# A decoder trunk on one core: two weight sums recorded later, and one block product moved up in the last up unit

## The chip, the cores and the metric

The kernel runs on one core of one Trainium2 chip. The metric is the device time of one execution in microseconds (us); for a kernel it is the median of its runs.

## What is computed

Two decoder layers over 1024 positions of width 1024, in float32. Each layer has a token mixer with four memory cross-attention heads beside it, an output projection, and a dense MLP:

```
def squared_relu_mlp(h, w_up, w_down):
    a = jax.nn.relu(h @ w_up)
    return (a * a) @ w_down
...
        x = x + jnp.concatenate([mix, cross], axis=-1) @ w_o[i]
        x = x + squared_relu_mlp(rmsnorm(x, mlp_norm_g[i]), mlp_w_up[i], mlp_w_down[i])
    return rmsnorm(x, final_norm_g)
```

`w_up` is 1024 x 4096 and `w_down` 4096 x 1024. Layer 0 has latent attention, layer 1 sliding-window attention; the change touches only the MLPs.

## The kernel before

**Precision.** TensorE multiplies operands that are rounded to float32r. Each float32 operand is split into a high part (ScalarE copies it into a float32r tile, line 99) and a low part (VectorE subtracts the high part, line 100), and each product is made of three matmuls: high by high, high by low, low by high (lines 1700 to 1702 in the up product, 2053 to 2055 in the down product).

**Strassen.** Both MLP products run as Strassen's seven block products on 2 x 2 blocks. The up product (function `mlp`) goes through 16 units `i` of 256 hidden columns. For a unit the raw weights come by two DMAs (`load_raw`, line 1619), are scaled by the norm's gain on ScalarE (`gain_w`, line 1592), and are combined on VectorE (`sum_w`): s1 = a21+a22 (line 1635), s2 = s1-a11 (1636), a21 = a11-a21 (1637) and s4 = a12-s2 (1638). `sums[i]` gives product `p` its weight block; `prep_w(i, p)` splits it, and `up_mm(i, p)` runs its twelve matmuls.

- Products 1, 6, 7 and 4 of a unit add up in the bank `psu`, products 2, 5 and 3 in a bank `psv`. `evac` copies `psu` out after products 1 and 6 and `psv` after product 5 (ScalarE, line 1743), since the later results need these values alone. The next product into that bank waits for the copy.
- After products 2, 7 and 3 VectorE adds a saved copy (line 1756) and squares (1735, in layer 1's first two units 1732 and 1733 on ScalarE). Products 3 and 4 end with sums of the hidden blocks (1766 to 1768 and 1748, 1751), and each block is written to DRAM (`hd`, line 1738). Line 1748 is the last reader of `psu`.
- There are two `psu` slots. Unit i+2 waits for line 1748 of unit i, and the second down tile `psy` takes the slot of the last unit.

**The order of the products.** `seq` lists (unit, product). The first two units go in turn through 6, 5, 7, 3, 4 (their products 1 and 2 ran earlier). Every later unit goes 1, 2, 6, 5, 7, 3, 4. The operand of product 6 (`X[6]`) lies in the tile `f0`, that of product 5 in `f1`; that of products 1 and 2 in `q0` and `q1`. Matmul rows name these tiles `mqf` (f0, f1) and `mqq` (q0, q1).

**From up to down.** In the last unit `dn.begin(p)` follows each product: after product 6 it loads the first eight down weight blocks into `f0` (four DMAs of 512 KB, line 1859), after product 5 the next eight into `f1`. A load waits until the last matmul that reads its tile has ended. The down product (class `Down`) then goes through (product, 256 rows) steps of 24 matmuls, with operands split four steps ahead.

**What sets the order.** The lines above are the order in which work is *recorded*. A scheduler then places each recorded instruction in its engine's queue by its own estimates of when the inputs are there, with earlier recorded work first among those that are ready. Each engine and the DMA queue of SP (SyncE) then works strictly in queue order. So moving a few lines can reorder neighbours that the lines don't name.

The lines that the prediction follows:

```
            G(a21, a11, a21, SUB)
            G(s4, a12, s2, SUB)
...
        seq += [(i, p) for i in range(2, NP) for p in (1, 2, 6, 5, 7, 3, 4)]
...
            go(i, p, ready.pop((i, p)))
            if i == NP - 1:
                dn.begin(p)
```

Of the kernel before, what the change touches and what calls it, by code (L numbers as in the profile page):

```python
# [55 lines left out]
def trunk(  # L56
# [39 lines left out]
    def split(src, hi, lo, scale=None):  # L96

        if scale is None:
            r = nc.scalar.activation(hi, src, AF.Copy)  # L99
            return r, nc.vector.tensor_tensor(lo, src, f32(hi), ALU.subtract)  # L100
        else:
            nc.scalar.activation(hi, src, AF.Copy, scale=scale)
            nc.vector.scalar_tensor_tensor(lo, src, scale, f32(hi), ALU.mult, ALU.subtract)
# [845 lines left out]
    def units_of(h):  # L949
        return units if h < H - 1 else units_end  # L950
# [153 lines left out]
    seq = [(h, u) for h in range(H) for u in units_of(h)]  # L1104
# [78 lines left out]
    NP = FF // 256  # L1183
    TORD = list(range(NT))
    SUB = ALU.subtract

    def k4(ap):
        return ap.rearrange("p (k c) -> p k c", k=4)
# [419 lines left out]
    def mlp(layer, m, early_w=None, early_mm=None):  # L1608

        X, xr = m.X, m.xr  # L1610
        V, G = nc.vector, nc.vector.tensor_tensor
# [6 lines left out]
            for h in range(2):  # L1618
                nc.sync.dma_start(out=r[h], in_=wsrc[:, 4 * h : 4 * h + 4, 256 * i : 256 * i + 256])

        ss = []

        def gain_w(i):
            for h in range(2):
# [2 lines left out]
        def sum_w(i):  # L1627
            if i < 2:
                ss.append([m.t(f"i{j}")[:, 0, :] for j in (1, 3, 5)] if i == 0 else [*[m.t("d2")] * 2, m.t("i7")[:, 0, :]])
                if i == 1:  # L1630
                    ss[1][0:2] = [ss[1][0][:, j, :] for j in range(2)]
            r = raws.pop(i)
            a11, a12, a21, a22 = r[0][:, :, 0:P], r[1][:, :, 0:P], r[0][:, :, P:256], r[1][:, :, P:256]
            s1, s2, s4 = [k4(a) for a in ss[i % 2]]
            G(s1, a21, a22, ALU.add)
            G(s2, s1, a11, SUB)
            G(a21, a11, a21, SUB)
            G(s4, a12, s2, SUB)
            sums[i] = {1: a11, 2: a12, 3: s4, 4: a22, 5: s1, 6: s2, 7: a21}

        def pair(t_):
# [21 lines left out]
        def prep_w(i, p):  # L1663
            a = sums[i][p]
            n = hct[0]
            hct[0] += 1
            if n < 7:
                hl.append([k4(v) for v in opens[n]()])
            hi, lo = hl[n % 7]
            split(a, hi, lo)  # L1670
            return hi, lo
# [6 lines left out]
        def prep_x(p, cols=range(4)):  # L1678
            for j in cols:
                c = slice(j * P, (j + 1) * P)  # L1680
                if layer and (p != 6 and j < 2 or len(cols) == 4):
                    if j % 2:
                        continue
                    c = slice(j * P, (j + 2) * P)
                src = m.t2[j] if p == 6 else xr[{5: 0, 7: 1, 4: 2, 3: 3}[p]][:, :, c]
                hi, lo = [v[:, :, c] for v in X[p]]
                split(src, hi, lo)
# [83 lines left out]
                write(7, i, h)  # L1771

        seq = [(i, p) for p in (6, 5, 7, 3, 4) for i in range(2)]
        seq += [(i, p) for i in range(2, NP) for p in (1, 2, 6, 5, 7, 3, 4)]
        LA = 4
        ready = {}

# [14 lines left out]
        else:  # L1792
            gain_w(0)
        sum_w(0)
        prep_x(6, range(3))
        load_raw(1)
# [5 lines left out]
        with tc.issue_after(m.last_n.ins):  # L1802
            gain_w(1)
        sum_w(1)
        ready[(1, 6)] = prep_w(1, 6)
        prep_x(5, (3,))
        ready[(0, 5)] = prep_w(0, 5)
        X[7] = [m.t("g0", F32R), m.t("g1", F32R)]
        X[3] = [m.t("g2", F32R), m.t("g3", F32R)]
        with tc.issue_after(m.last_n.ins):  # L1810
# [8 lines left out]
        for n, (i, p) in enumerate(seq):  # L1819
            for q_ in seq[n : n + LA]:  # L1820
                if q_ not in ready:
                    ready[q_] = prep_w(*q_)
            if (i, p) == (1, 7):
                load_raw(2)
                gain_w(2)
                sum_w(2)
            if p == 4 and 0 < i < NP - 2:
                load_raw(i + 2)
            if p == 2 and i < NP - 1:
                gain_w(i + 1)  # L1830
            if p == 6 and 2 <= i < NP - 1:
                sum_w(i + 1)
# [3 lines that stand above are left out]
# [341 lines left out]

    jw, early = {}, []
    mlp(0, m0, lambda: jw.update(early_w()), early_mm)
    m0.rp.release()  # L2180
    kv1p = pool("kv1p")
# [183 lines left out]
    m1 = Mlp(1, x1)  # L2365
    wo_strassen(1, wq, [f0, f1], m1)
    mlp(1, m1)
    m1.rp.release()
    m1.s.release()
# [35 lines left out]
```

## Time and profile before

| | us |
|---|---|
| median of 3 runs | 2110.15 |
| the runs | 2110.25, 2110.15, 2108.54 |
| the profiled execution, its own time | 2112.17 |
| its span (first to last instruction) | 2110.5 |
| TensorE busy in the span | 2071.6 (98%) |
| VectorE busy | 1493.9 (71%) |
| ScalarE busy | 1142.9 (54%) |

The profiled execution took 2.02 us more than the median and 1.7 us more than its own span. "Busy" counts an instruction from its start to its end; since matmuls overlap, TensorE can show 98% while single waits of a microsecond remain.

### The profile page before, as it was taken

Reading aid. Unit: us, or ns where it says so; the run is one execution under the profiler, and the core shown is the slowest. Engines: PE = TensorE matmul, PEld = TensorE weight load, DVE = VectorE, ACT = ScalarE, POOL = GpSimd, SP = SyncE. Lnnn points to the kernel's source line nnn. Section 1 sums busy time; section 2 is a strip of 40 time slices with the busy share of each in tenths; the row PEclk is TensorE's granted clock in tenths of the full one; section 3 lists DMA queues with packets and bytes.
Section 4 is the critical chain, followed back from the end, with each engine's and each line's share of the span. In section 5 each row is a group of like instructions: output and inputs, shape, how many; then the busy total and the mean of one; then the engine's idle time right before and its main releaser. Section 6 shows DMA issues by size and latency. Waiting matters only on the chain.

```text
span 2110.5 us, 29217 instructions
## 1 busy us (share of the span) xinstructions
PE 2071.6 (98%) x9880; PEld 1699.8 (81%) x9880; DVE 1493.9 (71%) x2876; ACT 1142.9 (54%) x2461; POOL 204.7 (10%) x288
## 2 busy tenths in 40 slices
PE   7999999999999999999999999999999999999998
PEld 6988778778778888788888878778788887888887
DVE  7555688865977766797667543897976775976565
ACT  5445477776744453444445553877845443444452
POOL 0013100000000000031111231631000000000000
PEclk9999999999999999999999999999999999999999
DMA  7202123343254445976653211146344446844332
GB/s 247 68 1 76 46 63 90 105 146 100 96 184 146 139 154 195 325 254 205 212 165 95 75 31 30 41 156 234 122 152 146 165 140 225 316 152 154 117 119 90
DMA packets 181632, 294.47 MB, mean 140 GB/s; under 512 B 18557, under 2 KB 74346, under 8 KB 181482
## 3 DMA queue, kind: packets, MB, share of 16 engines
q1 hardware_dynamic: 171008, 264.25, 38.9%
q0 software_dynamic: 8048, 25.70, 3.5%
q10 hardware_dynamic: 2426, 2.65, 0.4%
q8 instruction: 78, 1.28, 0.2%
q14 instruction: 72, 0.59, 0.1%
HBM read 194.81 MB, written 85.25 MB: 133 GB/s over the span
## 4 chain that ended last, share of the span: by engine, by line
PE 76%; DVE 8%; DMA 8%; ACT 5%; issue 2%; SPq 0%; POOL 0%; DVEq 0%; ACTq 0%; POOLq 0%
PE psy L2053 5%; PE psy L2055 5%; PE psy L2054 5%; PE psz L2054 4%; PE psz L2053 4%; PE psz L2055 4%; PE pss L964 4%; PE pso L1006 3%; PE psu L1700 3%; PE psu L1702 3%; PE psu L1701 3%; DMA mr<-in_mlp_w_up_dram 3%; DMA d<-in_mlp_w_up_dram 3%; PE psf L108 2%; PE psf L110 2%; PE psf L109 2%
## 5 line engine op out<-in xcount | busy, mean ns | idle before, releaser
L1592 ACT ACTIVATE mr<-mr,gcol 128x256 f32<-128x256 f32 (+1 forms) x160 | 67.7, 479 | 79.0 <-DMA mr<-in_mlp_w_up_dram 64.4
L2053 PE MATMUL psy<-g 128*128 128x512 f32 x256 | 99.9, 390 | 0.0
L2054 PE MATMUL psy<-g 128*128 128x512 f32 x256 | 99.6, 389 | 0.0
L2055 PE MATMUL psy<-g 128*128 128x512 f32 x256 | 99.3, 389 | 0.0
L1592 ACT ACTIVATE d<-d,gcol 128x256 f32<-128x256 f32 x128 | 57.3, 499 | 75.5 <-DMA d<-in_mlp_w_up_dram 65.4
L99 ACT ACTIVATE g<-i 128x512 fp32r<-128x512 f32 x79 | 49.6, 628 | 88.3 <-PE psz L2054 41.2
L99 ACT ACTIVATE i<-mr 128x512 fp32r<-128x512 f32 x86 | 54.0, 628 | 68.6 <-PE psz L2054 20.0
L985 ACT ACTIVATE p<-pss 128x512 f32<-128x512 f32 x108 | 63.6, 593 | 41.1 <-PE pss L964 41.0
L100 DVE TENSOR_TENSOR g<-i,g 128x512 fp32r<-128x512 f32 x79 | 55.6, 704 | 40.7 <-ACT g L99 40.6
L99 ACT ACTIVATE uh<-i 128x512 fp32r<-128x512 f32 x66 | 41.6, 630 | 76.9 <-PE psy L2054 35.7
L100 DVE TENSOR_TENSOR pl<-p,ph 128x512 fp32r<-128x512 f32 (+1 forms) x96 | 61.6, 651 | 27.6 <-ACT ph L99 27.1
L839 DVE TENSOR_REDUCE m<-psx 128x1 f32<-128x128 f32 (+5 forms) x96 | 70.2, 748 | 11.0 <-PE psx L835 10.8
L2053 PE MATMUL psz<-g 128*128 128x512 f32 x192 | 74.7, 389 | 0.0
L2054 PE MATMUL psz<-g 128*128 128x512 f32 x192 | 74.7, 389 | 0.0
L2055 PE MATMUL psz<-g 128*128 128x512 f32 x192 | 74.7, 389 | 0.0
L100 DVE TENSOR_TENSOR uh<-i,uh 128x512 fp32r<-128x512 f32 x66 | 45.5, 689 | 36.7 <-ACT uh L99 36.7
L100 DVE TENSOR_TENSOR i<-mr,i 128x512 fp32r<-128x512 f32 x78 | 53.6, 687 | 21.2 <-ACT i L99 21.0
L99 ACT ACTIVATE ph<-p 128x512 fp32r<-128x512 f32 (+1 forms) x96 | 56.4, 599 | 1.3
L1928 DVE TENSOR_TENSOR mqf<-mqq,mqf 128x512 f32<-128x512 f32 x64 | 43.0, 687 | 19.3 <-DMA mqq<-in_mlp_w_down_dram 19.2
L2055 PEld LDWEIGHTS psy<-g 128*128 128x128 f32 x256 | 48.0, 188 | 10.0
L2053 PEld LDWEIGHTS psy<-g 128*128 128x128 f32 x256 | 48.1, 188 | 9.9
L2054 PEld LDWEIGHTS psy<-g 128*128 128x128 f32 x256 | 48.1, 188 | 9.8
(746 smaller groups left out, 6972.8 us busy)
## 6 DMA issues: line engine op xcount, KB each, us to landing
i<-hd SPq DMA_DIRECT2D x154, 256.0 KB
hd<-uh SPq DMA_DIRECT2D x76, 256.0 KB
hd<-ul SPq DMA_DIRECT2D x76, 256.0 KB
mr<-in_mlp_w_up_dram SPq DMA_DIRECT2D x36, 512.0 KB
hd<-x SPq DMA_DIRECT2D x72, 256.0 KB
mr<-hd SPq DMA_DIRECT2D x70, 256.0 KB
d<-in_mlp_w_up_dram SPq DMA_DIRECT2D x32, 512.0 KB
mqq<-in_mlp_w_down_dram SPq DMA_DIRECT2D x32, 512.0 KB
```

The source lines that it names most:

```text
L99: r = nc.scalar.activation(hi, src, AF.Copy)
L100: return r, nc.vector.tensor_tensor(lo, src, f32(hi), ALU.subtract)
L839: nc.vector.reduce_max(m8s[h][:, i : i + 1], ps[:, c], axis=AX, negate=True)
L964: return lambda: nc.tensor.matmul(o, a, b, skip_group_check=True, **kw)
L985: nc.scalar.activation(p, ps, AF.Exp, scale=SC)
L1006: mms.append(lambda: nc.tensor.matmul(o, a, b, skip_group_check=True, **kw))
L1592: nc.scalar.activation(w[:, k, :], w[:, k, :], AF.Copy, scale=g_mlp[layer][:, k0 + k : k0 + k + 1])
L1700: nc.tensor.matmul(ps, wh[:, k, :], xh[:, k, :], start=p in (1, 2, 5) and k == 0, stop=False, skip_group_check=True)
L1701: nc.tensor.matmul(ps, wh[:, k, :], xl[:, k, :], start=False, stop=False, skip_group_check=True)
L2053: nc.tensor.matmul(ps, ah[:, j, :], bh, start=p in (1, 5, 2) and k == 0, stop=False, skip_group_check=True)
L2054: nc.tensor.matmul(ps, ah[:, j, :], bl, start=False, stop=False, skip_group_check=True)
L2055: nc.tensor.matmul(ps, al[:, j, :], bh, start=False, stop=k == NP - 1, skip_group_check=True)
```

## The change

In the first up unit (i = 0, in both layers) the last two weight sums, lines 1637 and 1638, are no longer recorded in `sum_w` but kept and recorded later: after the splits for products 6 of units 0 and 1 and product 5 of unit 0. In the last up unit (i = 15) the products go 1, 6, 2, 5, 7, 3, 4 instead of 1, 2, 6, 5, 7, 3, 4.

```diff
@@ sum_w @@
             G(s1, a21, a22, ALU.add)
             G(s2, s1, a11, SUB)
-            G(a21, a11, a21, SUB)
-            G(s4, a12, s2, SUB)
+
+            def rest():
+                G(a21, a11, a21, SUB)
+                G(s4, a12, s2, SUB)
+
+            if i:
+                rest()
+            else:
+                held.append(rest)
@@ mlp @@
         seq = [(i, p) for p in (6, 5, 7, 3, 4) for i in range(2)]
-        seq += [(i, p) for i in range(2, NP) for p in (1, 2, 6, 5, 7, 3, 4)]
+        seq += [(i, p) for i in range(2, NP) for p in ((1, 2, 6, 5, 7, 3, 4) if i < NP - 1 else (1, 6, 2, 5, 7, 3, 4))]
...
         ready[(0, 5)] = prep_w(0, 5)
+        held[0]()
         X[7] = [m.t("g0", F32R), m.t("g1", F32R)]
```

Line numbers after the change are 2 to 8 higher: 1637 and 1638 become 1639 and 1640; 1700 to 1702 become 1707 to 1709; 1738, 1748, 1756 and 1766 become 1745, 1755, 1763 and 1773; 1859 becomes 1867.

In the queues, layer 0 is unchanged on every engine up to its last up unit. The layers' last units change in the same way; layer 0's is shown. On PE, `psu_15` takes product 1 (weights `i_0_99`, `i_0_100`, operand `mqq`) and then product 6 (operand `mqf`), `psv_15_2` product 2. Before:

```order
L1701 MATMUL psu_15_7849<-mqq_0_32_5152,i_0_99_5819 128x512
L1702 MATMUL psu_15_7849<-mqq_0_32_5152,i_0_100_5820 128x512
L1700 MATMUL psv_15_2_7865<-mqq_0_33_5153,i_0_101_5823 128x512
L1701 MATMUL psv_15_2_7865<-mqq_0_33_5153,i_0_101_5823 128x512
L1702 MATMUL psv_15_2_7865<-mqq_0_33_5153,i_0_102_5824 128x512
L1700 MATMUL psv_15_2_7865<-mqq_0_33_5153,i_0_101_5823 128x512
L1701 MATMUL psv_15_2_7865<-mqq_0_33_5153,i_0_101_5823 128x512
L1702 MATMUL psv_15_2_7865<-mqq_0_33_5153,i_0_102_5824 128x512
L1700 MATMUL psv_15_2_7865<-mqq_0_33_5153,i_0_101_5823 128x512
```

Now:

```order
L1708 MATMUL psu_15_7849<-mqq_0_32_5152,i_0_99_5819 128x512
L1709 MATMUL psu_15_7849<-mqq_0_32_5152,i_0_100_5820 128x512
L1707 MATMUL psv_15_2_7885<-mqq_0_33_5153,x_0_105_5871 128x512
L1708 MATMUL psv_15_2_7885<-mqq_0_33_5153,x_0_105_5871 128x512
L1709 MATMUL psv_15_2_7885<-mqq_0_33_5153,x_0_105_5871 128x512
L1707 MATMUL psv_15_2_7885<-mqq_0_33_5153,x_0_105_5871 128x512
L1708 MATMUL psv_15_2_7885<-mqq_0_33_5153,x_0_105_5871 128x512
L1707 MATMUL psu_15_7849<-mqf_0_78_5664,i_0_101_5823 128x512
L1708 MATMUL psu_15_7849<-mqf_0_78_5664,i_0_101_5823 128x512
```

Five of product 2's twelve matmuls still stand between products 1 and 6; the other seven follow product 6, and then product 5.

On SP, in the same unit: `mqf_0_138` is f0 with the first eight down blocks, `mqf_0_139` f1, `mqq_0_149` a further down block, and `hd_4817<-x` the write of product 2's result. Before:

```order
L1859 DMA mqq_0_149_7987<-in_mlp_w_down_dram 128x2x512
L1918 DMA i_0_143_7925<-hd_4817 128x512
L1738 DMA hd_4817<-x_0_111_5995 128x512
L1859 DMA mqq_0_149_7987<-in_mlp_w_down_dram 128x2x512
L1859 DMA mqf_0_138_7896<-in_mlp_w_down_dram 128x2x512 x4
L1859 DMA mqf_0_139_7917<-in_mlp_w_down_dram 128x2x512 x4
L1738 DMA hd_4820<-x_0_111_5995 128x512
```

Now:

```order
L1867 DMA mqq_0_149_7987<-in_mlp_w_down_dram 128x2x512
L1926 DMA i_0_143_7925<-hd_4817 128x512
L1867 DMA mqf_0_138_7878<-in_mlp_w_down_dram 128x2x512 x4
L1745 DMA hd_4817<-x_0_111_5995 128x512
L1867 DMA mqf_0_139_7917<-in_mlp_w_down_dram 128x2x512 x4
L1745 DMA hd_4820<-x_0_111_5995 128x512
```

The write and the second `mqq` load no longer stand ahead of f0's four loads; the second `mqq` load comes some 35 rows later. On ScalarE the first split of f0 (`i_0_165<-mqf`) now also stands ahead of the copy of product 5 (`i_0_77<-psv_15_5`), which it followed before.

On VectorE, the same unit, from the third split of a down operand to line 1748 (`ul_106<-psu_15`), which frees the slot for `psy`. Before:

```order
L100 TENSOR_TENSOR g_0_167_8018<-mqf_0_138_7896,g_0_167_8018 128x512
L1756 TENSOR_TENSOR x_0_111_5995<-psv_15_5_7903,i_0_76_5662 128x512
L100 TENSOR_TENSOR g_0_168_8023<-i_0_141_7923,g_0_168_8023 128x512
L1735 SCALAR_TENSOR_TENSOR x_0_111_5995<-x_0_111_5995 128x512
L100 TENSOR_TENSOR g_0_168_8023<-mqf_0_138_7896,g_0_168_8023 128x512
L1766 TENSOR_TENSOR uh_82_5697<-x_0_111_5995 128x512
L100 TENSOR_TENSOR g_0_169_8028<-i_0_142_7924,g_0_169_8028 128x512
L1767 TENSOR_TENSOR uh_82_5697<-uh_82_5697,x_0_111_5995 128x512
L1768 TENSOR_TENSOR x_0_111_5995<-x_0_111_5995 128x512
L1748 TENSOR_TENSOR ul_106_5918<-psu_15_7849,ul_106_5918 128x512
```

Now (line 1755 is the former 1748):

```order
L1742 SCALAR_TENSOR_TENSOR x_0_111_5995<-x_0_111_5995 128x512
L100 TENSOR_TENSOR g_0_167_8018<-mr_140_7922,g_0_167_8018 128x512
L100 TENSOR_TENSOR g_0_167_8018<-mqf_0_138_7878,g_0_167_8018 128x512
L1763 TENSOR_TENSOR x_0_111_5995<-psv_15_5_7903,i_0_76_5662 128x512
L100 TENSOR_TENSOR g_0_168_8023<-mqf_0_138_7878,g_0_168_8023 128x512
L1742 SCALAR_TENSOR_TENSOR x_0_111_5995<-x_0_111_5995 128x512
L100 TENSOR_TENSOR g_0_169_8028<-i_0_142_7924,g_0_169_8028 128x512
L1773 TENSOR_TENSOR uh_82_5697<-x_0_111_5995 128x512
L1755 TENSOR_TENSOR ul_106_5918<-psu_15_7849,ul_106_5918 128x512
```

Lines 1767 and 1768 no longer come ahead of it, and the split `g_0_168<-i` has moved further up; on PE six matmuls into the second `psy` tile have moved up from the 15th place of the down product to the 8th.

In layer 1 the beginning of the up product changes too. On SP, `mr_81` and `mr_82` are the two halves of unit 2's raw weights, `d_86` and `d_87` those of unit 3. Before:

```order
L1619 DMA mr_81_13653<-in_mlp_w_up_dram 128x4x256
L1619 DMA mr_82_13654<-in_mlp_w_up_dram 128x4x256
L1619 DMA d_1_86_13755<-in_mlp_w_up_dram 128x4x256
L1738 DMA hd_4820<-ul_80_13646 128x512
L1619 DMA d_1_87_13756<-in_mlp_w_up_dram 128x4x256
```

Now:

```order
L1619 DMA mr_81_13653<-in_mlp_w_up_dram 128x4x256
L1619 DMA d_1_86_13755<-in_mlp_w_up_dram 128x4x256
L1745 DMA hd_4820<-ul_80_13646 128x512
L1619 DMA mr_82_13654<-in_mlp_w_up_dram 128x4x256
L1619 DMA d_1_87_13756<-in_mlp_w_up_dram 128x4x256
```

The second half of unit 2 now stands behind unit 3's first half and behind the write of unit 0's product 7 (`hd_4820<-ul_80`). On VectorE, from the sums of unit 2 (1635 to 1638) to line 1748 of unit 0 (`x_1_85<-psu_0`); `psv_0_5` and `psv_1_5` hold product 3 of units 0 and 1, `i_1_76` is the low part for unit 2's product 2. Before:

```order
L1635 TENSOR_TENSOR i_1_58_13467<-mr_81_13653,mr_82_13654 128x512
L1756 TENSOR_TENSOR uh_83_13699<-psv_0_5_13602,i_1_49_13385 128x512
L1636 TENSOR_TENSOR i_1_59_13468<-i_1_58_13467,mr_81_13653 128x512
L1637 TENSOR_TENSOR mr_81_13653<-mr_81_13653 128x4x128
L1638 TENSOR_TENSOR i_1_60_13469<-mr_82_13654,i_1_59_13468 128x512
L1756 TENSOR_TENSOR ul_84_13703<-psv_1_5_13618,i_1_50_13386 128x512
L1766 TENSOR_TENSOR uh_83_13699<-uh_83_13699,ul_80_13646 128x512
L100 TENSOR_TENSOR i_1_76_13560<-mr_82_13654,i_1_75_13559 128x512
L1767 TENSOR_TENSOR ul_84_13703<-uh_83_13699,uh_56_13437 128x512
L1768 TENSOR_TENSOR uh_83_13699<-uh_56_13437,uh_83_13699 128x512
L1766 TENSOR_TENSOR x_1_85_13727<-ul_84_13703,ul_80_13646 128x512
L1748 TENSOR_TENSOR x_1_85_13727<-psu_0_13410,x_1_85_13727 128x512
```

Now:

```order
L1635 TENSOR_TENSOR i_1_58_13467<-mr_81_13653,mr_82_13654 128x512
L1636 TENSOR_TENSOR i_1_59_13468<-i_1_58_13467,mr_81_13653 128x512
L1639 TENSOR_TENSOR mr_81_13653<-mr_81_13653 128x4x128
L1640 TENSOR_TENSOR i_1_60_13469<-mr_82_13654,i_1_59_13468 128x512
L1773 TENSOR_TENSOR uh_83_13699<-uh_83_13699,ul_80_13646 128x512
L1773 TENSOR_TENSOR x_1_85_13727<-ul_84_13703,ul_80_13646 128x512
L1774 TENSOR_TENSOR ul_84_13703<-uh_83_13699,uh_56_13437 128x512
L1775 TENSOR_TENSOR uh_83_13699<-uh_56_13437,uh_83_13699 128x512
L1774 TENSOR_TENSOR x_1_85_13727<-x_1_85_13727,uh_56_13437 128x512
L1775 TENSOR_TENSOR ul_84_13703<-uh_56_13437,ul_84_13703 128x512
L100 TENSOR_TENSOR i_1_76_13560<-mr_82_13654,i_1_75_13559 128x512
L1755 TENSOR_TENSOR x_1_85_13727<-psu_0_13410,x_1_85_13727 128x512
```

The rows of product 3 (1763 for `psv_0_5` and `psv_1_5`) now stand directly ahead of these twelve, all four sums of unit 2 behind them, and the split `i_1_76` is the eleventh of the twelve instead of the eighth. On PE, unit 2 of layer 1 now begins with two matmuls of product 2, two of product 5 and three of product 2, ahead of its product 1.

## Rows read from the trace of the kernel before

**Rows 1.** Waits on PE, whole span: us in total, times, longest.

```profile
PE psu L1700 <- ACT d L1743: 3.3, 7, 1.4
PE psy L2053 <- DVE ul L1748: 2.0, 2, 1.0
```

**Rows 2.** Timeline of PE, layer 0's last unit: start, us, ..., [idle before <-releaser].

```profile
840.17 0.39 PE L1700 MATMUL psu<-mqf,x 128*128 128x512 f32 x1
842.89 0.39 PE L1700 MATMUL psv<-mqf,x 128*128 128x512 f32 x1
...
851.35 0.50 PE L1700 MATMUL psu<-x,d 128*128 128x512 f32 x1
...
854.25 0.39 PE L2053 MATMUL psy<-i,i 128*128 128x512 f32 x1
...
858.57 0.50 PE L2053 MATMUL psy<-i,i 128*128 128x512 f32 x1 [0.99 <-DVE ul L1748]
```

**Rows 3.** Timeline of ACT, the same stretch.

```profile
837.96 0.58 ACT L1743 ACTIVATE d<-psu 128x512 f32<-128x512 f32 x1
845.87 0.60 ACT L1743 ACTIVATE i<-psv 128x512 f32<-128x512 f32 x1 [2.12 <-PE psv L1702]
849.34 0.63 ACT L99 ACTIVATE i<-mqf 128x512 fp32r<-128x512 f32 x1 [2.87 <-DMA mqf<-in_mlp_w_down_dram]
```

**Rows 4.** Timeline of DVE, the same stretch.

```profile
850.00 0.69 DVE L100 TENSOR_TENSOR i<-mqf,i 128x512 fp32r<-128x512 f32 x1 [8.22 <-ACT i L99]
...
857.83 0.68 DVE L1748 TENSOR_TENSOR ul<-psu,ul 128x512 f32<-128x512 f32 x1
```

**Rows 5.** Timeline of SP's DMA queue, the same stretch.

```profile
841.81 0.32 SPq L1738 DMA_DIRECT2D hd<-x  x1
842.18 0.43 SPq L1859 DMA_DIRECT2D mqq<-in_mlp_w_down_dram  x1
843.08 5.82 SPq L1859 DMA_DIRECT2D mqf<-in_mlp_w_down_dram  x8
```

**Rows 6.** Windows: length, busy us of PE, PEld, DVE, ACT, POOL; PEclk, DMA share, GB/s.

```profile
843.00:849.00 6.00, 6.00 (x28) 4.96 (x27) 0.00 (x0) 1.20 (x2) 0.00 (x0) 1.00 0.90 301
1496.00:1498.00 2.00, 2.00 (x7) 1.52 (x6) 2.00 (x4) 2.00 (x3) 0.00 (x0) 0.50 0.00 0
```

**Rows 7.** Timeline of PE, layer 1's last unit and first down step.

```profile
1793.82 0.50 PE L1700 MATMUL psu<-x,d 128*128 128x512 f32 x1 [0.31 <-DVE x L1756]
1801.03 0.50 PE L2053 MATMUL psy<-i,i 128*128 128x512 f32 x1 [1.03 <-DVE ul L1748]
```

**Rows 8.** Timeline of PE, units 0 to 2: layer 0, then layer 1.

```profile
582.43 0.50 PE L1700 MATMUL psu<-mqq,i 128*128 128x512 f32 x1 [0.42 <-DVE x L1748]
...
1494.59 0.49 PE L1700 MATMUL psu<-mqf,i 128*128 128x512 f32 x1 [1.31 <-ACT mqf L99]
1495.86 0.63 PE L1702 MATMUL psu<-mqf,i 128*128 128x512 f32 x1
1498.85 0.45 PE L1700 MATMUL psu<-mqf,i 128*128 128x512 f32 x1
...
1524.14 0.39 PE L1700 MATMUL psu<-mqq,i 128*128 128x512 f32 x1
```

**Rows 9.** Timeline of SP's DMA queue, layer 1's units 0 to 2.

```profile
1511.05 0.37 SPq L1619 DMA_DIRECT2D d<-in_mlp_w_up_dram  x1
1513.59 0.34 SPq L1738 DMA_DIRECT2D hd<-ul  x1
```

**Rows 10.** Timeline of ACT, the same stretch.

```profile
1514.00 1.71 ACT L1592 ACTIVATE mr<-mr,gcol 128x256 f32<-128x256 f32 x4 [0.44 <-DMA mr<-in_mlp_w_up_dram]
```

**Rows 11.** Timeline of DVE, the same stretch.

```profile
1515.74 0.69 DVE L1635 TENSOR_TENSOR i<-mr,mr 128x512 f32<-128x512 f32 x1 [1.13 <-ACT mr L1592]
...
1518.90 0.69 DVE L1756 TENSOR_TENSOR ul<-psv,i 128x512 f32<-128x512 f32 x1
...
1522.52 0.68 DVE L1748 TENSOR_TENSOR x<-psu,x 128x512 f32<-128x512 f32 x1
```

More of the change, by code (lines that the diff above doesn't have):

```diff
@@ L1619, in load_raw @@
                 nc.sync.dma_start(out=r[h], in_=wsrc[:, 4 * h : 4 * h + 4, 256 * i : 256 * i + 256])
-        ss = []
+        ss, held = [], []
         def gain_w(i):
```

## The prediction

> **What bounds the kernel now.** I read the page first: TensorE (PE) is busy nearly throughout, so the time is PE's work plus PE's waits, and a change that adds and removes no matmul can only move waits. The list of PE's waits comes second [rows 1]: two entries concern this change. The second tile of the down product, `psy`, waits twice (once a layer, 2.0 us in all) for line 1748, and products that share `psu` wait for ScalarE's copies. Third come the timelines of layer 0's last unit on PE, ScalarE, VectorE and SP [rows 2 to 5]. Twelve matmuls of a product take 842.89 - 840.17 = 2.72 us, or 0.227 each [rows 2]. Read the queues together: SP issues the first `f0` load at 843.08, as soon as product 6 has let go of the tile [rows 5]; ScalarE's split of it starts 6.26 us later and had waited 2.87 us for the DMA [rows 3]; VectorE's half of that split starts at 850.00 after 8.22 us of idling, because everything else stands behind it in its queue [rows 4]. From there it works thirteen instructions off, one each 0.60 us, to line 1748 at 857.83, and `psy` waits 0.99 us for that one [rows 2]. So the wait at the seam is a late weight load, passed on by two queues.
>
> Layer 1's seam reads the same, with 0.31 and 1.03 us [rows 7]. Last I read the start of layer 1's up product [rows 8 to 11], since the queues move there too. From 1498.85 to unit 2's start at 1524.14 the list has no wait of PE.
>
> **The change part by part.** Nothing is removed or added: the same splits, sums, matmuls and DMAs. I price moves only.
>
> *Held sums, layer 0.* Its queues are as before on all engines up to the last unit, so this part costs nothing and gives nothing there; no cover is needed, since no row moves.
>
> *Product 6 second, both layers.* Without any wait, products 5, 7 and 3 from 842.89 would bring product 4 to 842.89 + 3 x 2.72 = 851.05 and the fifteenth down matmul to 851.05 + 26 x 0.227 = 856.95. It started at 858.57 [rows 2]. So 1.62 us a layer is all that can be won at the seam. What it takes:
>
> - Product 2 begins at 840.17 - 2.72 = 837.45 in the old order. Now five of its matmuls fill 1.13 us after product 1, and product 6 begins at 838.58. It adds into the bank that product 1's copy reads; that copy ran from 837.96 to 838.54 [rows 3]. The cover just reaches; I allow 0.1 us. Were the five not there, 1.1 us would be lost.
> - Product 6's last matmul ends near 841.5 instead of 843.0, so `f0`'s loads start at about 841.6, 1.5 us sooner. That is seven matmuls, not a whole product.
> - Ahead of them in SP's queue a write (841.81) and a 512 KB load (842.18) are gone [rows 5], 768 KB together. With the load's old delay of 6.26 us the first block would be there at 847.9. If nothing but those 768 KB held it back, at the 301 GB/s of that stretch [rows 6] they cost 2.5 us, and it would be there at 845.4. I take 846.8, a bit on the early side of the middle, because the DMA share was 0.90 there, so bytes ahead did cost time.
>
> The Trainium skill, "DMA: Bandwidth & Descriptors", section "Queues, rings and completion order", says that within one ring descriptors are consumed in the order in which they were queued. By that rule the write and the load ahead delay `f0` in full and the loads behind it do not, which would give the early end, 845.4, and the whole 1.6 us a layer; no row here separates the ring's order from the mere sharing of bandwidth.
>
> - Now the price. ScalarE's first split of `f0` stands ahead of the copy of product 5 now, where that copy ran freely at 845.87 [rows 3]. Product 3 adds into the same bank and is due at 848.33, so split and copy (0.54 and 0.58 us, and 0.05 to wake) must be through: no loss if the block is there by 847.2. At 846.8 there is none; at 847.9 it is 0.7 us.
> - VectorE then starts its backlog some 2.5 us sooner, is held by product 7's end (about 848.5), and reaches line 1755, now the eleventh after the first split, at 848.6 + 10 x 0.60 = 854.6, and is done at 855.3. `psy`'s second tile is due after seven matmuls, at 851.05 + 19 x 0.227 = 855.36. That just fits; another 0.1 us allowed.
> - The second `mqq` load comes later, behind which nothing waits early: its reader is a sum many steps on.
>
> That gives 1.4 us a layer, with ends 0.7 and 1.6: **2.8 us gained** in two layers (1.4 to 3.2).
>
> *Layer 1's start.* Here the order pays something back.
>
> - The second half of unit 2's raw weights was issued near 1510.0, just ahead of the load of 1511.05; ScalarE got it at 1514.00 [rows 9, 10]. Now it stands behind the write of unit 0's product 7, which was issued at 1513.59 [rows 9] and hangs on ScalarE's squares. So it goes out at about 1513.7 and lands near 1517.9 to 1518.5. Scaling takes 1.71 us [rows 10]: ready at 1519.6 to 1520.2.
> - VectorE did unit 2's four sums from 1515.74 on, in the time that it had to wait for product 3 of unit 1 (1518.90) [rows 11]. Now they stand behind that row and find their input at about 1519.9. Line 1755 of unit 0 is the twelfth row from there: it starts at 1519.9 + 11 x 0.60 = 1526.5 and ends at 1527.2; before, it started at 1522.52 [rows 11]. The split `i_1_76` ahead of it ends at 1526.6.
> - PE reaches unit 2 at 1524.14 [rows 8]. Four matmuls are ready, to 1525.05. The fifth needs `i_1_76`: 1.6 us of waiting, then three matmuls to 1527.3, and product 1 needs line 1755 done. Together **1.7 us lost**.
>
> The nearest row from below is layer 0's same seam, where unit 2 waited 0.42 us for line 1748 [rows 8]; from above, 1.9 us by the later landing, plus what the clock may take. In layer 1 a wait of 1.31 us was followed by a granted clock of 0.50 (1.2 instead of 2.4 GHz) [rows 6, 8], and matmuls then started every (1498.85 - 1495.86) / 7 = 0.43 us; nine such cost 9 x 0.2 = 1.8 us. After the waits of 0.99 and 1.03 us the first matmul took 0.50, not 0.63 [rows 2, 7]. I leave the clock out of the sum and make it a rival. That early wait itself stays: as many VectorE rows as before precede the split it waits for. So nothing is gained here.
>
> Sum: 1.7 - 2.8 = -1.1 us. Against the profiled execution's own 2112.17 that is 2111.1; that execution lay 2.0 us above the median of the runs, 2110.15, which I take as the base: **2109.1 us**.
>
> **The rivals.**
>
> - *No payback in layer 1.* The load lands sooner or PE finds other work: 0.4 us as in layer 0. For it: the scheduler itself put other products ahead there. Against: twelve VectorE rows after 1518.90 leave no room. -2.8 + 0.4 = -2.4: 2107.8.
> - *The clock falls after the new wait.* For it: 1.6 us exceeds the 1.31 after which it fell. Against: there a second wait of 0.3 followed at once. -1.1 + 1.8 = +0.7: 2110.9.
> - *The load moves half of what I take.* The block is there at 847.9 in each layer: -1.4 + 1.7 = +0.3: 2110.5.
> - *Slower: ScalarE is held in front of product 5's copy.* The place is the first split of `f0`. If the block lands no sooner than before (849.34), the copy ends at 850.5, product 3 starts 2.2 us late, and the seam loses 2.2 - 1.4 = 0.8 us a layer. It decides from a landing at 848.6 on, where 1.4 us are lost. For it: the DMA share there is 0.90, and an earlier start may only mean a longer queue. Against: less is queued ahead. +1.6 + 1.7 = +3.3: 2113.5.
> - *The change does not do what it says.* For the sums in layer 0 this is so by the queues; for the loads it is the third rival, or the fourth.
>
> **How the numbers follow.** Forecast 0.50; no payback 0.17; clock 0.15; half 0.08; slower 0.10. The range 2106.8 to 2112.6 takes in the first four with about 1 us to either side for the terms' ends (the three runs shown lie 1.7 us apart), and leaves out the slower case. About 0.2%, or 4.2 us, is what a measurement can tell from no change here, so all five cases lie within it. Faster than that needs no payback and the early fall of the clock gone as well (another -1.8): 0.04. Slower needs the fourth rival and the clock: 0.06. Same: 0.90.
>
> **What would show it.** In the profile after: the first `f0` load is issued about 1.5 us sooner after product 1's end; ScalarE's wait for it ends 2 to 3 us sooner; the two waits of `psy` for the line 1755 shrink to 0.2 us or less; the copy of product 5 follows the split without making product 3 wait. In layer 1, unit 2 shows a new wait of about 1.6 us for VectorE, with the granted clock at 1.0. I am wrong if product 3 waits for ScalarE by over 0.7 us, if unit 2 starts without a wait, or if some later unit waits for weights that now come late.

## The result and the profile after

The change makes the kernel slower: median 2115.54 us of 14 runs (2112.07 to 2120.01) against 2109.06 of 14 runs before, ratio 1.0027 with a 95% interval of 1.002 to 1.0035. Predicted was 2109.1, in 2106.8 to 2112.6.

| us | before | after |
|---|---|---|
| median of 14 runs | 2109.06 | 2115.54 |
| profiled execution, its span | 2112.17, 2110.5 | 2116.95, 2115.2 |
| TensorE busy | 2071.6 | 2073.6 (98%) |
| VectorE, ScalarE busy | 1493.9, 1142.9 | 1494.4, 1142.2 |
| layer 1: first up matmul to unit 5's product 1 | 104.5 | 110.7 |
| last units: product 1 to the first `ul,uh` matmul of `psy` | 31.7, 31.9 | 30.6, 30.2 |

The last two lines are differences of starts on PE's timeline. The profile before was an execution 3.1 us above the median of its runs, the one after 1.4 above, so the profiles differ by 4.8 and the medians by 6.5.

The list of PE's waits after, beside [rows 1] (waited for: us in total, times, longest):

```profile
PE psu L1707 <- ACT d L1750: 4.5, 11, 1.2
PE psv L1709 <- DVE i L100: 2.0, 1, 2.0
PE psv L1707 <- ACT x L99: 0.8, 1, 0.8
PE psv L1707 <- ACT i L99: 0.4, 1, 0.4
PE psy L2061 <- DVE ul L1755: 0.2, 1, 0.2
```

The two waits of `psy`, 2.0 us, have shrunk to one of 0.2: the seams gained. The three `psv` waits, 3.2 us, are new and all stand at unit 2 of layer 1. The copies' waits of `psu` come at other units than before, in layer 0 too, where no row moved before its last unit; part of them is scatter of single executions. In all eleven profiles of this document layer 0's rows stand in the same order up to there, and from product 1 of unit 2 to product 1 of unit 15 they took 251.6 to 254.3 us.

Layer 0's seam after, from the timelines of PE, SP, ScalarE and VectorE (this profile is about 1.9 us later here than the one before):

```profile
844.87 0.39 PE L1707 MATMUL psv<-mqf,x 128*128 128x512 f32 x1
857.67 0.50 PE L2061 MATMUL psy<-i,i 128*128 128x512 f32 x1 [0.18 <-DVE ul L1755]
...
843.48 1.92 SPq L1867 DMA_DIRECT2D mqf<-in_mlp_w_down_dram  x4
...
847.29 0.63 ACT L99 ACTIVATE i<-mqf 128x512 fp32r<-128x512 f32 x1 [3.15 <-DMA mqf<-in_mlp_w_down_dram]
847.85 0.60 ACT L1750 ACTIVATE i<-psv 128x512 f32<-128x512 f32 x1
...
856.94 0.68 DVE L1755 TENSOR_TENSOR ul<-psu,ul 128x512 f32<-128x512 f32 x1
```

The first `f0` block is there 847.29 - 843.48 = 3.81 us after its issue, against 6.26 before [rows 3, 5]. It is the shortest of sixteen such flights in the eight profiles with the loads moved up; the others took 4.1 to 4.9 us. The copy of product 5 follows the split at once and holds nobody up. Line 1755 ends 0.05 us before `psy` goes on.

Layer 1's start after. First SP's DMA queue (`d`: unit 3's raw halves, `mr`: the second half of unit 2), then ScalarE, VectorE and PE:

```profile
1511.63 0.38 SPq L1619 DMA_DIRECT2D d<-in_mlp_w_up_dram  x1
1512.99 0.34 SPq L1745 DMA_DIRECT2D hd<-ul  x1
1513.42 0.39 SPq L1619 DMA_DIRECT2D mr<-in_mlp_w_up_dram  x1
...
1519.93 1.71 ACT L1592 ACTIVATE mr<-mr,gcol 128x256 f32<-128x256 f32 x4 [2.01 <-DMA mr<-in_mlp_w_up_dram]
...
1512.12 0.68 DVE L100 TENSOR_TENSOR d<-mr,d 128x512 fp32r<-128x512 f32 x1
...
1521.68 0.69 DVE L1635 TENSOR_TENSOR i<-mr,mr 128x512 f32<-128x512 f32 x1 [2.46 <-ACT mr L1592]
...
1527.83 0.68 DVE L100 TENSOR_TENSOR i<-mr,i 128x512 fp32r<-128x512 f32 x1
...
1524.30 0.50 PE L1707 MATMUL psv<-mqq,i 128*128 128x512 f32 x1 [0.38 <-ACT i L99]
1525.82 0.50 PE L1707 MATMUL psv<-mqf,x 128*128 128x512 f32 x1 [0.79 <-ACT x L99]
1528.57 0.79 PE L1709 MATMUL psv<-mqq,i 128*128 128x512 f32 x1 [2.01 <-DVE i L100]
1530.01 0.63 PE L1707 MATMUL psu<-mqq,i 128*128 128x512 f32 x1
```

Read it as a chain. VectorE's split `d<-mr,d` of 1512.12 is the last reader of the buffer that the half is loaded into. Before, it stood ahead of product 7's results in VectorE's queue and ran at 1509.28; the second of the two loads, 0.38 us long, went out at about 1510.0, right behind it:

```profile
1504.25 6.13 SPq L1619 DMA_DIRECT2D mr<-in_mlp_w_up_dram  x2
...
1509.28 0.69 DVE L100 TENSOR_TENSOR d<-mr,d 128x512 fp32r<-128x512 f32 x1
```

So the buffer comes free 2.8 us later; the load goes out at 1513.42, 3.4 us later than before; and it lands at 1519.93, 5.9 us later [rows 10], since it flies 6.5 us where it flew 4.0. Everything behind it waits in a row: scaling, sums, splits, PE. Of the 3.4 us, 0.6 is the write `hd` of 1512.99, which now goes ahead of the load. And layer 1 began 0.4 us later in this profile (1477.17 against 1476.75), so 0.4 us of each of the three delays is not the change's; the flights are free of it.

The windows of that place show the rest (columns as in [rows 6]):

```profile
1526.00:1528.00 2.00, 0.56 (x2) 0.12 (x2) 2.00 (x5) 2.00 (x6) 0.00 (x0) 1.00 1.03 379
1528.00:1530.00 2.00, 1.43 (x3) 1.16 (x4) 2.00 (x4) 1.41 (x3) 0.00 (x0) 0.64 1.00 372
1530.00:1532.00 2.00, 2.00 (x6) 1.60 (x5) 2.00 (x4) 0.00 (x0) 0.00 (x0) 0.51 0.75 283
1532.00:1534.00 2.00, 2.00 (x10) 1.62 (x10) 1.92 (x4) 0.35 (x1) 0.00 (x0) 1.00 0.69 242
```

Behind the three waits the granted clock is at 1.2 GHz from 1528.57 to just before 1532 (0.64 and 0.51 in two windows, then 1.00). The three matmuls from 1528.57 take 1.44 us instead of 0.68, the twelve of product 1 (1530.01 to 1533.68 on PE's timeline) 3.67 instead of 2.72: 1.7 us lost.

### The profile page after: what moved, and what is told of

It reads as the page before. It is cut to its first block, busy times and chain, and to the rows that moved or that the text cites. A ratio compares the mean times of both kernels' runs of the same rounds, so it can differ in the third digit from the quotient of the medians.

```text
span 2115.2 us, 29221 instructions
## 1 busy us (share of the span) xinstructions
PE 2073.6 (98%) x9880; PEld 1699.1 (80%) x9880; DVE 1494.4 (71%) x2876; ACT 1142.2 (54%) x2461; POOL 206.1 (10%) x288
## 4 chain that ended last, share of the span: by engine, by line
PE 69%; DVE 10%; DMA 9%; ACT 5%; issue 5%; POOL 1%; SPq 0%; DVEq 0%; ACTq 0%; POOLq 0%
PE psy L2063 5%; PE psy L2062 5%; PE psy L2061 5%; PE psz L2063 4%; PE psz L2062 4%; PE psz L2061 4%; DMA mr<-in_mlp_w_up_dram 4%; PE pss L964 4%; PE pso L1006 3%; DMA d<-in_mlp_w_up_dram 3%; PE psu L1707 3%; PE psu L1708 2%; PE psu L1709 2%; PE psf L108 2%; PE psf L110 2%
## 5 line engine op out<-in xcount | busy, mean ns | idle before, releaser
L2062 PEld LDWEIGHTS psy<-g 128*128 128x128 f32 x256 | 48.1, 188 | 9.9
L2061 PEld LDWEIGHTS psy<-g 128*128 128x128 f32 x256 | 48.1, 188 | 9.9
```

The source lines that it names most:

```text
L2061: nc.tensor.matmul(ps, ah[:, j, :], bh, start=p in (1, 5, 2) and k == 0, stop=False, skip_group_check=True)
L2062: nc.tensor.matmul(ps, ah[:, j, :], bl, start=False, stop=False, skip_group_check=True)
```

## The experiments

Theory after the result: the seams' gain is real, and all of the loss lies at layer 1's start and hangs on the late landing of unit 2's second half. Rivals: the loss is spread; or VectorE's new order is enough for it without the load.

### Each half of the change alone

In seq_only the order of the last units alone is changed:

```diff
-        seq += [(i, p) for i in range(2, NP) for p in (1, 2, 6, 5, 7, 3, 4)]
+        seq += [(i, p) for i in range(2, NP) for p in ((1, 2, 6, 5, 7, 3, 4) if i < NP - 1 else (1, 6, 2, 5, 7, 3, 4))]
```

In held_only this line stays as before and the sums are held as in the change.

> The last up units go 1, 6, 2, 5, 7, 3, 4 as in the change; the two sums stay where they were. Theory: the whole loss lies at the start of layer 1's up product and comes from the held sums; the two seams into the down product gain 1.3 us each, as the profile after shows. Then this kernel takes 2109.1 - 2.6 = 2106.5 us (2105.5 to 2107.5), and unit 2 of layer 1 starts without a wait. Rival: the new order of the last units costs something elsewhere (layer 0 lay 2.3 us later than before already ahead of its seam): then 2108 to 2111.

Measured: 2107.57 us, just above the expected range, ratio to before 0.9989 (0.9979 to 0.9998). Unit 2 of layer 1 starts without a wait, and one wait of `psy`, 0.20 us, is left.

> The two sums are held; the last units keep their order. Theory: all of the loss and none of the gain: 2115.5 + 2.6 = 2118.1 us (2116.5 to 2119.5), the waits of unit 2 in layer 1 as in the change (3.2 us and then a lower clock), and the two waits of psy back at about 1 us each. Rival (the loss is spread, the seams' gain isn't real in the median): 2113 to 2116.

Measured: 2116.89 us, ratio 1.0035 (1.0022 to 1.0047). The load and its landing, PE's waits at unit 2, `psy`'s, and the clock behind:

```profile
1510.88 0.39 SPq L1619 DMA_DIRECT2D mr<-in_mlp_w_up_dram  x1
...
1518.05 1.71 ACT L1592 ACTIVATE mr<-mr,gcol 128x256 f32<-128x256 f32 x4 [2.63 <-DMA mr<-in_mlp_w_up_dram]
...
1522.41 0.50 PE L1707 MATMUL psv<-mqq,i 128*128 128x512 f32 x1 [0.99 <-ACT i L99]
1523.93 0.50 PE L1707 MATMUL psv<-mqf,x 128*128 128x512 f32 x1 [0.79 <-ACT x L99]
1526.68 0.80 PE L1709 MATMUL psv<-mqq,i 128*128 128x512 f32 x1 [2.01 <-DVE i L100]
...
PE psy L2061 <- DVE ul L1755: 1.9, 2, 1.0
...
1528.00:1530.00 2.00, 2.00 (x6) 1.52 (x6) 2.00 (x4) 0.00 (x0) 0.00 (x0) 0.53 0.73 275
```

The two halves separate cleanly: the order gains, the held sums lose, and each half brings its own waits of the full change. By the stretch from layer 1's first up matmul to unit 5 the held sums cost 6.5 us (111.0 against 104.5 both before and in seq_only). By the medians against the kernel before, the halves are worth -1.6 and +7.7 us, 6.1 together, near the 6.5 of both at once.

### Is the late split the first link?

held_early_split is the change and these two lines:

```diff
+            if layer and (i, p) == (1, 5):
+                ready[(0, 4)] = prep_w(0, 4)
             go(i, p, ready.pop((i, p)))
```

> The change as it is, and in layer 1 the split of unit 0's weights for product 4 is recorded two steps earlier. That split is the last reader of the buffer into which the second half of unit 2's raw weights is loaded; VectorE's queue has it ahead of product 7's result again. Theory: the late split is the first link (split 2.8 us late, load 3.4 us late, landing 5.9 us late, sums, split, PE): with it early the load goes out near 1510, unit 2 waits under 0.5 us and the time is that of the order of the last units alone, 2106.5 us (2105.5 to 2108). Rival: VectorE's order behind product 3's results is enough by itself: unit 2 still waits 1.5 us or more and the time stays over 2110.

Measured: 2109.07 us, ratio 0.9994 (0.9983 to 1.0004). The split that frees the buffer (here `i<-mr,i`) now ends at 1507.34, and VectorE, SP, ScalarE and PE show:

```profile
1506.65 0.69 DVE L100 TENSOR_TENSOR i<-mr,i 128x512 fp32r<-128x512 f32 x1
...
1502.23 5.53 SPq L1619 DMA_DIRECT2D mr<-in_mlp_w_up_dram  x2
...
1512.35 1.70 ACT L1592 ACTIVATE mr<-mr,gcol 128x256 f32<-128x256 f32 x4
...
1522.52 0.39 PE L1707 MATMUL psv<-mqq,i 128*128 128x512 f32 x1
1523.20 0.39 PE L1707 MATMUL psu<-mqq,i 128*128 128x512 f32 x1
```

Both loads of unit 2 have gone out by 1507.76, ScalarE no longer waits for the second, and unit 2 starts with no wait, with the sums still held. So the late split is the first link, and at layer 1's start holding the sums does harm only by it: the stretch to unit 5 takes 104.9 us. The rival falls. The median is 1.1 us above the expected range; this execution's granted clock also fell at 1493 (as in the profile before) and near 1314, where nothing differs from the other kernels (it did so in seq_again and seq_x_first too). Why the median keeps 1.5 us on seq_only stays open.

### Why does the load fly 6.5 us?

held_load3_later is the change, and unit 3's loads are put behind unit 2's second half:

```diff
+                if layer and i == 1:
+                    with tc.issue_after(m.lr.ins):
+                        load_raw(3)
+                else:
+                    load_raw(i + 2)
```

`m.lr` is the DMA of unit 2's second half. PE's queue is that of the change, row for row.

> The change as it is, and in layer 1 unit 3's raw loads stand behind unit 2's second half in SP's queue; PE's queue is word for word that of the change. Theory: the half took 6.5 us to land instead of 4.0 because a 512 KB load of unit 3 went 1.8 us ahead of it and another 0.5 us behind; alone it is there 4 us after an issue at 1512.8, 3 us sooner, the waits of unit 2 shrink from 3.2 to about 1 us and the time from 2115.5 to about 2112 (2110.5 to 2113.5; lower by up to 2 more if the clock stays up). Rival: the landing has other reasons (the half lands 6 us after its issue here too): 2114.5 or more.

Measured: 2111.6 us, ratio 1.0008 (0.9999 to 1.0017). SP, ScalarE, PE, and the window behind the wait:

```profile
1502.02 8.63 SPq L1619 DMA_DIRECT2D mr<-in_mlp_w_up_dram  x2
1510.74 0.46 SPq L1745 DMA_DIRECT2D hd<-ul  x1
1511.24 0.42 SPq L1619 DMA_DIRECT2D d<-in_mlp_w_up_dram  x1
...
1514.50 1.71 ACT L1592 ACTIVATE mr<-mr,gcol 128x256 f32<-128x256 f32 x4 [0.65 <-DMA mr<-in_mlp_w_up_dram]
...
1523.60 0.50 PE L1709 MATMUL psv<-mqq,i 128*128 128x512 f32 x1 [1.39 <-DVE i L100]
...
1524.00:1526.00 2.00, 2.00 (x10) 1.63 (x9) 2.00 (x5) 1.62 (x4) 0.00 (x0) 1.00 0.83 307
```

The second issue ends at 1510.65, so it began near 1510.26 (0.39 long), and the half is there 4.2 us later. With unit 3's 512 KB and the 256 KB write queued ahead of it the same load took 6.5 us (the change), 7.2 (held_only: 1510.88 to 1518.05) and 7.0 (the change's second profile, below). Without them it took 4.0 to 4.2 in the six profiles in which ScalarE waited for it. So that order of the queue costs 2.3 to 3.2 us. How much of it is the 768 KB ahead is not quite separated: in the change unit 3's second half also stood 0.5 us behind, and the run moved that too. PE waits once, 1.39 us, and the clock stays up: 3.9 us of the median come back by moving two DMAs (the write went behind the half with them).

### Is the seam's gain in the loads or in the products' order?

seq_loads_behind_p2 is seq_only, and the loads go behind product 2:

```diff
-            if i == NP - 1:
+            if i == NP - 1 and p == 2:
+                with tc.issue_after(m.lw.ins):
+                    dn.begin(6)
+            elif i == NP - 1 and p != 6:
                 dn.begin(p)
```

`m.lw` is the write of product 2's result.

> The order 1, 6, 2, 5, 7, 3, 4 in the last units as in the kernel seq_only, PE's queue word for word the same, but the first eight down blocks stand behind product 2's write and the second mqq load in SP's queue, as before the change. Theory: the seam's gain comes from the loads going out sooner, not from the products' order. Product 2 now ends 1.6 us after product 6, so the loads go out 3 to 4 us later than in seq_only; psy's second tile waits 0.5 to 2.5 us for the line that frees its slot, and the time rises from 2107.6 to 2110 (2108.5 to 2112.5). Rival: the order of the products alone does it; then it stays at 2107.6 and psy waits no longer than 0.2 us.

Measured: 2109.82 us, ratio 0.9999 (0.9991 to 1.0008). SP, ScalarE and PE of layer 0, then of layer 1:

```profile
844.38 5.62 SPq L1862 DMA_DIRECT2D mqf<-in_mlp_w_down_dram  x8
849.33 0.63 ACT L99 ACTIVATE i<-mqf 128x512 fp32r<-128x512 f32 x1 [0.47 <-DMA mqf<-in_mlp_w_down_dram]
854.95 0.50 PE L2056 MATMUL psy<-i,i 128*128 128x512 f32 x1
...
1790.37 0.63 ACT L99 ACTIVATE i<-mqf 128x512 fp32r<-128x512 f32 x1 [1.48 <-DMA mqf<-in_mlp_w_down_dram]
1795.99 0.50 PE L2056 MATMUL psy<-i,i 128*128 128x512 f32 x1 [1.04 <-DVE ul L1748]
```

The median is where it was expected, but for half of the reason: by the ratios it lies about 2.1 us above seq_only, and `psy` waits 1.04 us. The other half was not found. Layer 0's block lands 4.0 us later after product 6 than in seq_only, and `psy` still does not wait: the scheduler moved line 1748 from the eleventh VectorE row behind the block's first split to the seventh (850.00 to 854.21, seven steps of 0.60), so it ends just as `psy` is due. In layer 1 the block flew 1.0 us longer (5.95 after its issue against 4.95), and `psy` waits 1.04: one for one. So the load's time decides once VectorE's slack is used up, and how much slack there is comes from the order of VectorE's rows. By the measure of the table above, layer 0's seam took 30.4 us (30.6 in seq_only) and layer 1's 31.4 (30.2): in layer 0 the rival is right, in layer 1 the loads are worth 1.2 us.

### Can the wait at layer 1's first product 6 go?

Every kernel so far waits there 1.3 and 0.3 us [rows 8]. seq_x_first is seq_only with the lines below and, in layer 1, the split of the last tile for product 6 directly behind its sum; seq_x_first_gain_later records `gain_w(1)` behind that split too.

```diff
         go(0, 1, m.fill[0][1])
+        if layer:
+            m.late[1]()
         go(0, 2, m.fill[0][2])
-        m.late[1]()
+        if not layer:
+            m.late[1]()
```

> seq_only, and in layer 1 the transposes of the last position tile are recorded ahead of product 2 of unit 0, with the split of the last quarter of product 6's operand right behind its sum. Theory: the wait of 1.3 and 0.3 us at the first product 6 of layer 1, which every kernel so far shows, ends with the ScalarE and VectorE chain from those transposes; the low part comes ninth instead of tenth in VectorE's queue, so the wait falls by about 0.6 us: 2107.0 (2106 to 2107.6). Where the clock stays up more often for it, up to 1 us less in the median. Rival: the chain's length stays and the moved work only comes due elsewhere: 2107.6 or more.

Measured: 2108.18 us, above the expected range, ratio 0.9996 (0.9987 to 1.0004).

> seq_x_first, and in layer 1 the scaling of unit 1's raw weights on ScalarE stands behind that split. Theory: the split's high part is ready about 0.9 us sooner on ScalarE, the first product 6 waits 0.6 to 1.0 us in all instead of 1.6: 2106.6 (2105.5 to 2107.5). Rival: unit 1's sums, now 2 us later, make product 6 or 5 of unit 1 wait, and the time is 2108 or more.

Measured: 2109.11 us, above the expected range too, ratio 0.9998 (0.9989 to 1.0006). In seq_x_first PE's timeline shows what took the wait's place:

```profile
1486.57 0.66 PE L1521 MATMUL psT_m<-ident,i 128*128 128x128 f32 x4 [2.46 <-ACT i L1511]
```

The waits at product 6 are gone in both, and PE waits 2.46 us for the transposes' input instead, ahead of which there were matmuls of product 2 before. The first rival holds: the wait moved up the chain, and from layer 1's first up matmul to unit 2's product 1 the kernels take 47.8 and 48.1 us, seq_only 47.1. Of the second rival the rows show only one new wait of 0.27 us, at a product 5.

### Once more, on one chip

> The change itself once more, for a second profile. Theory: the three waits at unit 2 of layer 1 (3.2 us in all) are the same in every execution, and the clock falls to half behind them here too, as in the two profiles that have them so far; the time is 2115.5 us (2114 to 2117). Rival: the fall is a chance of single executions, as it is behind the wait of 1.3 and 0.3 us at the first product 6 of layer 1 (2 of 9 profiles so far); then the clock may stay at full speed behind unit 2's waits, and this profile's span is about 2 us shorter.

Measured: 2115.29 us, ratio 1.003 (1.0019 to 1.004). The load and its landing, PE and the windows at unit 2:

```profile
1514.39 0.39 SPq L1619 DMA_DIRECT2D mr<-in_mlp_w_up_dram  x1
...
1521.37 1.71 ACT L1592 ACTIVATE mr<-mr,gcol 128x256 f32<-128x256 f32 x4 [2.31 <-DMA mr<-in_mlp_w_up_dram]
...
1525.73 0.50 PE L1707 MATMUL psv<-mqq,i 128*128 128x512 f32 x1 [0.83 <-ACT i L99]
1527.25 0.50 PE L1707 MATMUL psv<-mqf,x 128*128 128x512 f32 x1 [0.79 <-ACT x L99]
1530.00 0.80 PE L1709 MATMUL psv<-mqq,i 128*128 128x512 f32 x1 [2.01 <-DVE i L100]
...
1530.00:1532.00 2.00, 2.00 (x5) 1.62 (x6) 2.00 (x4) 0.84 (x2) 0.00 (x0) 0.50 0.98 366
1532.00:1534.00 2.00, 2.00 (x8) 1.59 (x7) 2.00 (x4) 0.00 (x0) 0.00 (x0) 0.65 0.75 281
```

The clock is at 1.2 GHz here too, as in all three profiles with these waits.

> The kernel seq_only once more, beside the change on one chip. Theory: faster than the kernel before by the two seams' 3.0 us less what runs scatter: 2107 (2106 to 2108.5), and 7 to 9 us faster than the change. Rival: the first 2107.6 was a lucky set of runs and the order alone is worth nothing in the median: 2109 or more.

Measured: 2106.85 us, ratio 0.9988 (0.998 to 0.9997): 8.4 us below the change on the same chip. The order of the last units without the held sums is faster than the kernel before by about 0.1% in both measurements, and than the change by 0.4%.

## Why the prediction was wrong

**The seams: right.** I put 1.4 us a layer, 2.8 in two. By the starts on PE the two seams are 1.1 and 1.6 us shorter, 2.7 in all. The loads went out when I said: just before product 5, 1.4 us ahead of its first matmul. The flight was shorter than the one I took. I let the 768 KB cost 1.1 of the 2.5 us and put the block at 846.8 (which lies on the late side of the middle of 845.4 and 847.9, not on the early side); on the old profile's clock it came at about 845.3, the early end. Other profiles put it later: with the write and the load just ahead (before, held_only) four flights took 5.8 to 6.4 us, without them sixteen took 3.8 to 4.9, half of them under 4.5. That is about 1.8 of the 2.5 us. The Trainium skill, "DMA: Bandwidth & Descriptors", section "Queues, rings and completion order", says that on each DMA engine descriptors are consumed in ring order. What I worked out from it, 845.4, agrees with this one seam; the middle of the sixteen flights is 0.7 us longer. The gain stayed under the 1.6 of that end, since VectorE's rows, not the load, then ended the wait of 0.18. That the earlier load was needed is shown for layer 1 alone: in layer 0 of seq_loads_behind_p2 another order of VectorE's rows did as well.

**Layer 1's start: the step that failed.** The step is "it goes out at about 1513.7 and lands near 1517.9 to 1518.5". The issue was right (1513.42). The landing was 1519.93, because I let the load fly as it had flown with nothing ahead of it. Now 768 KB stood ahead, the same amount that I had priced at up to 2.5 us at the seam a few lines earlier, and it flew 2.5 us longer. I priced one side of the same effect and not the other. How far the rest of the step holds, held_load3_later shows: with a flight of 4.2 us unit 2 waits 1.39 us, where I had written 1.6.

From the late landing follow two things that the sum did not have:

- The first four matmuls of unit 2, which I took as ready, waited too (0.38 and 0.79 us), since ScalarE's splits for them stand behind the scaling of the late half. That makes 3.2 us of waits instead of 1.6.
- The clock fell behind them: 1.7 us. It was my second rival with a price of 1.8, and I gave it 0.15, arguing from a single wait of 1.6.

A third part is smaller. Units 3 and 4 of layer 1 take 39.5 us instead of 38.1 before, 39.0 to 39.5 in all four profiles that have the sums held and the split late, and 38.1 with the early split. PE's timeline after lists two waits of `psu` for copies there, 0.19 and 0.24 us, too little for all of it; which delay of unit 3 makes the rest was not tried.

So layer 1's start cost 6.2 us by the table above instead of 1.7. By the starts on PE, unit 2 slipped by 5.6 us (3.2 idle, 1.7 for the clock, 0.7 for getting going after the waits) and units 3 and 4 by 1.4, while units 0 and 1 took 0.8 less than in the profile before: 6.2. The low clock that the profile before had at 1496 [rows 6] does not spoil the comparison: seq_only and seq_again, whose clock stayed up there, show 104.5 and 104.4 us for the same stretch.

**What stays open.** The named places add up to 3.5 us (6.2 lost, 2.7 gained), and the medians lie 6.5 apart (6.2 in change_again). With layer 1's start and the base put right, the forecast would be about 2112.5, still 3 us short. A part may be the clock in other executions: its mean over the runs of the change is 0.9970 and 0.9965 (14 and 12 runs), over those of the kernel before 0.9979 and 0.9978 (23 to 32 runs). The difference of about 0.0011 is, as an estimate, 2.3 us of 2115, and 1.7 of them are the fall at unit 2. The rest, about 2 us, was not located: both measurements have it, but a single profile scatters by as much where no row moved, so two profiles can't show where it lies.

**The base.** I took the first three runs' median, 2110.15; with 14 runs it is 2109.06, 1.1 less.

**The rivals.** The slower one, ScalarE held in front of product 5's copy, did not come: the copy followed the split at 847.85. The forecast's sentence that would show it wrong was "if some later unit waits for weights that now come late", and that is what unit 2 did, by more than the term had.

**What the held sums were worth.** They leave VectorE's queue ahead of the first product 6 of layer 1, but other splits take their two places, so the low part of the last quarter is the tenth row behind line 1512 before and after, and the wait of 1.3 and 0.3 us is the same in both.

## What to carry to other kernels

When a row moves down a queue, look for what it is the *last reader* of: a split that looks idle may be what lets the next load go out, and the price is paid a unit later. Price a transfer by the bytes queued shortly ahead of it (here up to 1.8 us ahead), in every place where the change alters them, the losing side as carefully as the winning. And test the halves of a change apart: one of these two gained and the other lost more than twice as much.

## What the runs showed of the hardware

- A 512 KB load with 768 KB issued 0.4 and 1.8 us ahead of it (and 512 KB 0.5 us behind) flew 6.5, 7.0 and 7.2 us; without them it flew 4.0 to 4.2 in six profiles, on the same buffer. At the seams, 512 KB issued 0.9 us and 256 KB 1.3 us ahead went with flights of 5.8 to 6.4 us; 512 KB issued 2.4 us and 256 KB 0.9 to 1.8 us ahead went with 3.8 to 4.9.
- TensorE's granted clock is not the same after the same waits. Nine profiles of these kernels show the wait of 1.3 and then 0.3 us at layer 1's first product 6; behind it the clock fell to 1.2 GHz in two of them (before and held_early_split) and stayed at 2.4 in seven. (The expectation of change_again says "2 of 9 so far", which counted the two kernels without that wait.) Behind the three waits of 3.2 to 3.8 us at unit 2 it fell in three of three, and behind single waits of 1.39 and 2.46 us it stayed up.
- Medians of the kernel before moved from 2109.06 to 2110.04 between measurements, and single runs by several us, so differences under 1 us were read from the rows and not from medians; rows of one profile scatter too, as layer 0's 251.6 to 254.3 us show.
